# Side loads of the first feed-forward layer moved from the sync queue to GpSimd's queue

## The chip, the cores and the metric

The kernel runs on one core of a Trainium2 chip. The metric is the device time of one execution in microseconds; the number for a kernel is the median of its runs. The profile is of one execution, with the times of all instructions on TensorE (PE, and PEld for its weight loads), VectorE (DVE), ScalarE (ACT), GpSimd (POOL) and the sync engine (SP), and of the DMA transfers.

## The reference, cut to what matters

Two model blocks run one after the other on 512 tokens (and 256 context tokens) of width 1024. The part that the change touches is the end of the first layer of the first block, and the side work that is done beside it:

```python
# first layer, both token groups (768 tokens in all)
h = h + m[5] * swiglu(modulate(rms_norm(h), m[3], m[4]), w_ffn_gate[0], w_ffn_up[0], w_ffn_down[0])
# swiglu(h, g, u, d) = (silu(h @ g) * (h @ u)) @ d       widths 1024 -> 2816 -> 1024

# parameters of the NEXT layer and of the second block: they depend on the conditions alone
m = silu(cond) @ w_ada[1] + b_ada[1]           # 6 x 1024 values, for c and for c_ctx
mod = silu(c_2) @ ada_w_2[0] + ada_b_2[0]      # the same for the second block
```

All arithmetic is in 32-bit floats. The matrix products are made as three products of a high and a low part.

## The kernel before

**The feed-forward layer.** `ffn` works through 22 blocks of 128 hidden columns in groups of 4, 4, 4, 4, 4 and 2 (`FFG`). For a block it loads one tile of `wgate` and one of `wup` (512 KB each), splits each into high and low (`wsplit`: a copy on ACT, L381, and a subtraction on DVE, L389), and makes two products of 768 tokens on PE (L434, L436, L439 are the three terms). `gated` then makes silu on ACT and the product on DVE, and splits that too. After a group come the down products: four tiles of `wdown` (512 KB), each split, each used for two output blocks, which DVE adds to the residual stream (L392).

**The side work.** `ada_rows` is a generator that computes the parameters of the next layer and of the second block on DVE: 96 tiles of `wadt` (128 rows of 1024 numbers, 512 KB each) are loaded, each is multiplied by the broadcast conditions (`cb`, loaded from `crow`) and summed along the row by one `scalar_tensor_tensor` at L672, or by two for the first 16 tiles of each 48. That makes 128 such instructions. `ffn` takes steps of the generator between its products (`self.step`): two before a block's first product, two before its second, two before each output block of the down products, from block 3 on.

**Memory.** All tiles come out of one arena, which gives out what was released longest ago. A load into a tile therefore waits until the last reader of the tile that lay there is done. Those readers are mostly DVE instructions.

**Order.** The program text gives dependencies and priorities. The framework's planner writes the order of the instructions on each engine and each queue from its own estimates, so that an engine's order is not that of the text. Each engine and each queue then works strictly in the written order, and waits at the head.

**Queues.** Every load, the weights' and the side work's, is issued by SP from `load` (L404 issues, L665 issues `crow`). GpSimd issues no DMA at all; its work near this stage is some additions and subtractions of the norms just before the layer (`norm_parts`) and just after it.

Of the kernel before, what the change touches and what calls it, by code (L numbers as in the profile page):

```python
# [359 lines left out]
class _K:  # L360
# [37 lines left out]
        self.nc.sync.dma_start(b.a, src)  # L398
        return b

    def load(self, src, top=False):
        shp = list(src.shape)
        b = self.A.new(shp[1:], top=top, parts=shp[0])
        self.nc.sync.dma_start(b.a, src)  # L404
        return b

    def split_to(self, hi, lo, f32, eng=None):
# [248 lines left out]
    def ada_rows(self):  # L656


        nc, A = self.nc, self.A
        cb = [A.new([1024], top=True) for _ in range(2)]  # L660
        for l in range(1, 3):
            P = self.P[l]
            for v in range(2):
                row = 2 * (l - 1) + v
                nc.sync.dma_start(cb[v].a, self.I["crow"][row:row + 1].to_broadcast([128, 1024]))  # L665
                self.act(cb[v].a, cb[v].a, AF.Silu)
            for n in range(48):
                w = self.load(self.I["wadt"][48 * (l - 1) + n])
                vs = range(2 if n < 16 else 1)
                for v in vs:  # L670
                    t = A.new([1024])
                    nc.vector.scalar_tensor_tensor(t.a, w.a, 1.0, cb[v].a, op0=OP.mult, op1=OP.mult,  # L672
                                                   accum_out=P.a[:, n, v:v + 1])
                    t.free()
                    if v == vs[-1]:
                        w.free()
                    yield
                if n % 16 == 15:
                    r = slice(n - 15, n + 1)
                    for v in vs:  # L680
                        self.tt(P.a[:, r, v], P.a[:, r, v], self.bada.a[:, l, r], OP.add)
                        for q in (8, 32):
                            if r.start <= q < r.stop:
                                nc.vector.tensor_scalar(P.a[:, q:q + 8, v], P.a[:, q:q + 8, v], 1.0, None, op0=OP.add)
        self.free(cb)
# [107 lines left out]
    def ffn(self, l, P, T, x, a, side, rate, start=0, hook=None):  # L793
# [36 lines left out]
        for g, nb in enumerate(FFG):  # L830
# [44 lines left out]
            if last and hook:  # L875
                ws = [load(u) for u in range(4)]
                for r in parts:
                    for u in range(4):
                        down(ws[u], u, [r])
                    hook()  # L880
                self.free(ws)
            else:
                for u in range(4):
                    w = load(u)
                    down(w, u, parts if two else [(0, T)])
                    self.free(w)
# [1934 lines left out]
```

## Time and profile before

| | |
|---|---|
| median of 3 runs | 3000.76 us (2995.12 to 3003.75) |
| profiled execution, its own time | 2993.29 us |
| its span, first to last instruction | 2991.6 us |
| mean granted clock of TensorE | 0.965 of full speed |
| PE busy | 2800.4 us (94% of the span) |
| the side work's loads | issued from 566.4 to 960.0 us |

The profiled execution is one of the faster ones: its own time lies 7.5 us below the median. Times inside the trace are counted from the start of the span.

### The profile page before, as it was taken

Reading aid. Unit: us, or ns where it says so; the run is one execution under the profiler, and the core shown is the slowest. Engines: PE = TensorE matmul, PEld = TensorE weight load, DVE = VectorE, ACT = ScalarE, POOL = GpSimd, SP = SyncE. Lnnn points to the kernel's source line nnn. Section 1 sums busy time; section 2 is a strip of 40 time slices with the busy share of each in tenths; the row PEclk is TensorE's granted clock in tenths of the full one; section 3 lists DMA queues with packets and bytes.
Section 4 is the critical chain, followed back from the end, with each engine's and each line's share of the span. In section 5 each row is a group of like instructions: output and inputs, shape, how many; then the busy total and the mean of one; then the engine's idle time right before and its main releaser. Section 6 shows DMA issues by size and latency. Waiting matters only on the chain.

```text
span 2991.6 us, 43517 instructions
## 1 busy us (share of the span) xinstructions
PE 2800.4 (94%) x17924; PEld 2038.1 (68%) x17924; DVE 1684.8 (56%) x2718; ACT 1042.4 (35%) x1730; POOL 261.4 (9%) x237
## 2 busy tenths in 40 slices
PE   7989999999999999999899999989898897999997
PEld 4877557888888887665588777877675574444343
DVE  5856547776576244676765775367965754221122
ACT  4522335511211226543553532246633533011011
POOL 0034320000000000122000000010000211000000
PEclk9999999999999999999999999989998998999998
DMA  6334452356466203111322222204212136999997
GB/s 222 105 106 113 137 182 94 117 200 210 147 220 208 67 26 109 41 32 38 109 78 85 85 85 71 79 22 148 78 51 78 50 108 246 420 422 421 421 421 283
DMA packets 145271, 458.97 MB, mean 153 GB/s; under 512 B 19585, under 2 KB 49921, under 8 KB 121137
## 3 DMA queue, kind: packets, MB, share of 16 engines
q1 hardware_dynamic: 145072, 456.20, 42.8%
q8 instruction: 140, 2.29, 0.3%
q14 instruction: 59, 0.48, 0.0%
HBM read 441.36 MB, written 14.79 MB: 152 GB/s over the span
## 4 chain that ended last, share of the span: by engine, by line
PE 67%; DVE 11%; DMA 5%; issue 4%; ACT 4%; POOL 0%; SPq 0%; DVEq 0%; ACTq 0%; POOLq 0%
PE ps L434 13%; PE ps L439 13%; PE ps L436 13%; PE ps L2676 9%; DVE mem L389 7%; ACT mem L381 4%; DMA mem<-in_wadt_dram 2%; PE ps L1624 1%; DMA mem<-in_eu_dram 1%; DVE mem L392 1%; PE ps L610 1%; PE ps L1119 1%; PE ps L1932 1%; PE ps L1587 1%; PE ps L1613 1%
## 5 line engine op out<-in xcount | busy, mean ns | idle before, releaser
L381 ACT ACTIVATE mem<-mem 128x1024 fp32r<-128x1024 f32 (+15 forms) x847 | 562.2, 695 | 844.2 <-PE ps L439 216.7
L389 DVE TENSOR_TENSOR mem<-mem,mem 128x1024 fp32r<-128x1024 f32 (+17 forms) x615 | 512.5, 849 | 361.8 <-ACT mem L381 175.8
L434 PE MATMUL ps<-mem,mem 128*128 128x512 f32 (+3 forms) x1991 | 599.0, 358 | 18.5 <-ACT mem L381 14.0
L381 ACT ACTIVATE mem<-ps 128x512 f32<-128x512 f32 (+9 forms) x614 | 310.0, 518 | 830.3 <-PE ps L439 320.3
L436 PE MATMUL ps<-mem,mem 128*128 128x512 f32 (+2 forms) x1906 | 568.7, 354 | 1.1 <-DVE mem L389 1.0
L439 PE MATMUL ps<-mem,mem 128*128 128x512 f32 (+2 forms) x1977 | 419.1, 353 | 0.0
L434 PEld LDWEIGHTS ps<-mem,mem 128*128 128x128 f32 (+2 forms) x1991 | 338.3, 189 | 86.6 <-ACT mem L381 20.2
L436 PEld LDWEIGHTS ps<-mem,mem 128*128 128x128 f32 (+1 forms) x1906 | 327.2, 189 | 60.7 <-issue 6.7
L439 PEld LDWEIGHTS ps<-mem,mem 128*128 128x128 f32 (+1 forms) x1977 | 325.1, 190 | 57.0 <-issue 4.1
L436 PE MATMUL ps<-mem 128*128 128x512 f32 (+1 forms) x862 | 284.9, 359 | 1.5 <-POOL mem L389 1.0
L389 DVE TENSOR_TENSOR mem<-mem,ps 128x512 f32<-128x512 f32 (+5 forms) x234 | 134.9, 605 | 261.0 <-PE ps L2676 127.2
L434 PE MATMUL ps<-mem 128*128 128x512 f32 (+1 forms) x777 | 268.2, 369 | 14.4 <-ACT mem L381 10.9
L389 DVE TENSOR_TENSOR mem<-mem 128x512 f32<-128x512 f32 (+24 forms) x373 | 195.9, 532 | 67.6 <-ACT mem L381 21.3
L389 POOL TENSOR_TENSOR mem<-mem 128x256 f32<-128x256 f32 (+4 forms) x72 | 96.8, 1346 | 1338.6 <-ACT mem L381 903.4
L2676 PE MATMUL ps<-mem,mem 128*64 128x512 f32 x784 | 209.1, 614 | 2.1 <-DMA mem<-in_eu_dram 1.8
L389 POOL TENSOR_TENSOR mem<-mem,mem 128x512 f32<-128x512 f32 (+6 forms) x88 | 119.3, 1364 | 993.8 <-ACT mem L381 870.5
L389 DVE TENSOR_TENSOR mem<-ps,mem 128x512 f32<-128x512 f32 (+6 forms) x212 | 134.4, 647 | 115.8 <-PE ps L1111 34.8
L2676 PE MATMUL ps<-mem 128*64 128x512 f32 x688 | 183.1, 606 | 1.7 <-DMA mem<-in_eu_dram 1.7
L439 PE MATMUL ps<-mem 128*128 128x512 f32 (+3 forms) x791 | 182.1, 356 | 0.0
L436 PEld LDWEIGHTS ps<-mem 128*128 128x128 f32 x862 | 159.7, 192 | 28.7 <-issue 2.7
L434 PEld LDWEIGHTS ps<-mem 128*128 128x128 f32 x777 | 146.1, 192 | 47.4 <-ACT mem L381 16.1
L392 DVE SCALAR_TENSOR_TENSOR mem<-ps,mem,mem 128x512 f32<-128x512 f32 (+2 forms) x130 | 78.7, 654 | 144.7 <-ACT mem L381 131.1
(303 smaller groups left out, 2936.3 us busy)
## 6 DMA issues: line engine op xcount, KB each, us to landing
mem<-in_eg_dram SPq DMA_DIRECT2D x64, 1024.0 KB, 19.7
mem<-in_eu_dram SPq DMA_DIRECT2D x64, 1024.0 KB, 19.5
mem<-in_ed_dram SPq DMA_DIRECT2D x56, 1024.0 KB, 19.4
mem<-in_wadt_dram SPq DMA_DIRECT2D x96, 512.0 KB, 4.4
mem<-in_wup_dram SPq DMA_DIRECT2D x44, 512.0 KB, 3.5
mem<-in_wgate_dram SPq DMA_DIRECT2D x44, 512.0 KB, 3.5
mem<-in_wdown_dram SPq DMA_DIRECT2D x40, 512.0 KB, 3.5
mem<-in_w2in_dram SPq DMA_DIRECT2D x35, 512.0 KB, 4.0
```

The costliest lines, as they stand in the source:

```text
L381: return self.nc.scalar.activation(out, in_, func, **kw)
L389: return (eng or self.nc.vector).tensor_tensor(out, a, b, op=op)
L392: return self.nc.vector.scalar_tensor_tensor(out, a, s, b, op0=op0, op1=op1)
L434: mm(o, w(0, k), acts[k][0][:, ts], start=(k == 0), stop=False)
L436: mm(o, w(0, k), acts[k][1][:, ts], start=False, stop=False)
L439: mm(o, w(1, k), acts[k][0][:, ts], start=False, stop=(k == nk - 1))
L610: nc.tensor.matmul(b.a[32 * q:32 * q + 32, :], cs.a[:, k, :], raw.a[:, j * 512:(j + 1) * 512], start=(k == 0), stop=(k == 7))
L1119: mm(out[half[i]], vv, w.a[:, i, :], start=(J == 0), stop=(J == last))
L1587: mm(b.a[:, t0:t1], qh.a[:96, i, 128 * c:128 * c + 128], kh.a[:96, i, t0:t1], start=True, stop=True)
L1613: mm(b.a, kh.a[:97, i, ks], qh.a[:97, i, :], start=True, stop=False)
L1624: m = mm(po.a[64 * i:64 * i + 64, :], v.a[:, kb, 64 * h:64 * h + 64], pt.a[:, i, :], start=(kb == 0), stop=(kb == 5))
L2676: mm(bk.a[64 * i:64 * i + 64, 512 * n:512 * n + 512], lhs(k, i), w[i][:, k % 2, 512 * n:512 * n + 512], start=(k == 0), stop=(k == 7))
```

## The change

`load` gets an argument that says which engine issues the transfer, and `ada_rows` passes GpSimd for the 96 loads of `wadt`. The four loads of `crow` in the same function stay on SP, and so do all weight loads. Tiles, sizes and arithmetic are the same.

```diff
-    def load(self, src, top=False):
+    def load(self, src, top=False, by=None):
         shp = list(src.shape)
         b = self.A.new(shp[1:], top=top, parts=shp[0])
-        self.nc.sync.dma_start(b.a, src)
+        (by or self.nc.sync).dma_start(b.a, src)
         return b
...
             for n in range(48):
-                w = self.load(self.I["wadt"][48 * (l - 1) + n])
+                w = self.load(self.I["wadt"][48 * (l - 1) + n], by=nc.gpsimd)
```

## Rows read from the trace of the kernel before

**Rows 1.** The page, part 4: the chain that ended last, shares of the span.

```profile
PE 67%; DVE 11%; DMA 5%; issue 4%; ACT 4%; POOL 0%; SPq 0%; DVEq 0%; ACTq 0%; POOLq 0%
PE ps L434 13%; PE ps L439 13%; PE ps L436 13%; PE ps L2676 9%; DVE mem L389 7%; ACT mem L381 4%; DMA mem<-in_wadt_dram 2%; PE ps L1624 1%; DMA mem<-in_eu_dram 1%; DVE mem L392 1%; PE ps L610 1%; PE ps L1119 1%; PE ps L1932 1%; PE ps L1587 1%; PE ps L1613 1%
```

**Rows 2.** Busy time of each engine in stretches; PEclk is the granted clock.

```profile
560.00:1000.00 440.00, 429.12 (x2441) 373.27 (x2440) 286.39 (x480) 92.78 (x124) 0.00 (x0) 0.99 0.57 188
...
700.00:750.00 50.00, 44.60 (x246) 38.52 (x245) 29.75 (x51) 8.69 (x10) 0.00 (x0) 0.93 0.52 173
...
800.00:850.00 50.00, 48.23 (x275) 41.68 (x275) 39.11 (x68) 8.97 (x11) 0.00 (x0) 1.00 0.48 158
...
900.00:950.00 50.00, 46.29 (x254) 39.91 (x253) 25.36 (x41) 9.30 (x12) 0.00 (x0) 0.97 0.59 176
```

**Rows 3.** Waits of PE, 560 to 1000 us: total, times, longest.

```profile
PE ps L434 <- ACT mem L381: 10.9, 3, 5.4
```

**Rows 4.** Waits of DVE, 560 to 1000 us, the longest group.

```profile
DVE mem L672 <- DMA mem<-in_wadt_dram: 76.9, 42, 4.8
```

**Rows 5.** The chain within 690 to 735 us: start, us, what.

```profile
691.41 5.65 DMA mem<-in_wadt_dram
...
698.41 4.18 DMA mem<-in_wadt_dram
...
703.95 4.27 DMA mem<-in_wadt_dram
...
711.91 5.21 DMA mem<-in_wdown_dram
...
721.32 1.65 PE ps L434 x4
```

**Rows 6.** The whole chain's longest pieces: first and last wadt load, one wdown load.

```profile
663.76 4.68 DMA mem<-in_wadt_dram
...
918.94 4.34 DMA mem<-in_wadt_dram
925.77 4.80 DMA mem<-in_wdown_dram
```

**Rows 7.** Waits of SP's queue, 560 to 1000 us, the two longest groups.

```profile
SPq L404 <- DVE mem L672: 192.9, 90, 8.5
SPq L404 <- DVE mem L389: 137.7, 47, 14.7
```

**Rows 8.** Timeline of SP, then of DVE, in order of time around 710 us.

```profile
710.77 0.33 SPq L404 DMA_DIRECT2D mem<-in_wadt_dram  x1
711.91 0.33 SPq L404 DMA_DIRECT2D mem<-in_wdown_dram  x1
...
709.51 1.22 DVE L672 SCALAR_TENSOR_TENSOR mem<-mem,mem 128x1024 f32<-128x1024 f32 x1
...
710.66 1.22 DVE L389 TENSOR_TENSOR mem<-mem,mem 128x1024 fp32r<-128x1024 f32 x1
```

**Rows 9.** DMA issues, 560 to 1000 us, below the dots 1330 to 1800: KB, median landing.

```profile
mem<-in_wadt_dram SPq DMA_DIRECT2D x96, 512.0 KB, 4.4
mem<-in_wdown_dram SPq DMA_DIRECT2D x20, 512.0 KB, 4.5
mem<-in_wup_dram SPq DMA_DIRECT2D x18, 512.0 KB, 4.2
mem<-in_wgate_dram SPq DMA_DIRECT2D x17, 512.0 KB, 4.5
...
mem<-in_wdown_dram SPq DMA_DIRECT2D x13, 512.0 KB, 3.4
```

**Rows 10.** The tile in_wadt_dram: its issues; min, median, max ns.

```profile
L404 SPq DMA_DIRECT2D mem<-in_wadt_dram x96: 327/328/961, 566.4 to 960.0; - x96
```

**Rows 11.** Timeline of POOL, 400 to 1150 us: the neighbours of the stage.

```profile
534.53 0.74 POOL L389 TENSOR_TENSOR mem<-mem 128x256 f32<-128x256 f32 x1 [16.07 <-ACT mem L381]
1105.62 4.05 POOL L389 TENSOR_TENSOR mem<-mem 128x512 f32<-128x512 f32 x3 [570.35 <-ACT mem L381]
```

## The prediction

> **What bounds the kernel now.** Begin with the chain of work that ended last [rows 1]. PE holds 67% of it, so the kernel as a whole is bound by matrix products, but one transfer of the side work is named too: loads of `wadt` are 2% of the span, some 63 us, on the chain. The change touches just these loads, so the next view is the stage in which they run. In the busy times by stretch [rows 2] PE works 429.1 of the 440 us from 560 to 1000, DVE 286.4, POOL nothing. The stage is PE's, with 10.9 us of stalls. The waits of PE name them all [rows 3]: three, the longest 5.4 us, each ended by an ACT copy, the first half of a weight split. One more thing is lost there: in two of the three 50 us stretches that hold a stall the granted clock is 0.93 and 0.97, in the third 1.00 [rows 2]. That is 50 x 0.07 + 50 x 0.03 = 5.0 us at the lower of the two levels (1.2 instead of 2.4 GHz) after PE had stood still. So the stage loses 10.9 + 5.0 = 15.9 us, which caps any gain here.
>
> Why is the split late? The reader should follow the chain into one stall [rows 5]: three `wadt` loads in a row, one after the other through DVE's L672, then a `wdown` load, the ACT copy that ends the stall, and PE at 721.32. DVE works in its written order and stands before an L672 whose tile has not landed; the subtraction of the split, further back in its queue, stands behind it. In all DVE waits 76.9 us, 42 times, for `wadt` [rows 4]. On the whole chain there are 14 long `wadt` pieces, from 663.76 to 918.94 us, seven ahead of the first stall, three ahead of the second, four ahead of the third [rows 6].
>
> Is it the queue that makes these loads late? SP's own waits say no [rows 7]. From 560 to 1000 us it waits 137 times for DVE at L672 or L389, 330.6 us in all, while 151 loads of `wadt` and weights go out (96 + 20 + 18 + 17 [rows 9]). So nearly every load stands at the head of the queue for its own release: the memory it will land in is still being read. The timeline shows it to the hundredth [rows 8]. The L672 that starts at 709.51 ends at 710.73 and the `wadt` load goes out at 710.77; the subtraction ends at 711.88 and the `wdown` load goes out at 711.91. What is left for the queue itself is the 14 or so loads without such a wait. A loop follows: load, land, L672, release, next load. Its length, not its queue, sets DVE's pace.
>
> **The change part by part.** *Removed from SP:* 96 issues of 0.33 us [rows 10], 31.7 us of SP's time. SP waits ten times as long in that stage [rows 7], so this is worth nothing. What hides it is that waiting.
>
> The Trainium skill (DMA: Bandwidth & Descriptors, "Issuing engines are not separate DMA queues") says that transfers issued from several engines run on the same 16 DMA engines, and that a second issuing engine saves only the sequencer's time to issue. By that rule alone the change would save the 31.7 us of SP's issue time and nothing on the path, so the sum would be 2993.3.
>
> *Added to POOL:* 96 issues, each behind the same release by DVE as before, on a queue that works in order. POOL issues no DMA in this trace, so the cost must be bounded. Below stands SP's 0.33 us [rows 10], no extra delay. Above stands POOL's mean for its instructions next to the stage, 4.05 / 3 = 1.35 us for 128x512 and 0.74 us for 128x256 [rows 11], so an extra of 0.4 to 1.0 us if an issue costs POOL about what its other instructions do. I take the middle of these two, 0.7 us, because an issue by POOL is program work on that engine like the others; the ends 0 and 1.0 stay for the range. In total POOL would be busy some 96 x 1.0 = 96 us of 440, with nothing else to do: its last work ahead of the stage is at 534.53, its next at 1105.62 [rows 11]. That is the cover; without it the norms would queue behind loads that wait for DVE.
>
> The extra delay sits inside the loop. Each of the 14 `wadt` pieces on the chain grows by it, and on the chain nothing hides it: 14 x 0.7 = 9.8 us (0 to 14). For the first stall alone that is 7 x 0.7 = 4.9 us. The other 82 loads grow as well. 42 waits end at a landing [rows 4], but today 76.9 us of such waits come out as 15.9 us lost, so most of DVE's waiting is soaked up before PE sees it; I count only those on the chain.
>
> The Trainium skill (DMA: Bandwidth & Descriptors, "Specifications") gives the first byte after about 1 us for a transfer that GpSimd issues and about 0.6 us from the sync queue. By its difference of 0.4 us the chain's term would be an estimated 5.6 us and the sum 2998.8. No run here shows it yet.
>
> *Moved:* the weight loads no longer share a queue with `wadt`. A `wdown` tile lands in 4.5 us in this stage and in 3.4 us in the second layer, where no side loads run [rows 9]. The two `wdown` loads on the chain took 5.21 and 4.80 us [rows 5, 6]. If a queue of their own lets them pass, they could win 1.8 + 1.4 = 3.2 us; if the DMA engines share themselves out as before, nothing. I take half, -1.6 us. The earliest issue of a weight load does not move, since it waits for DVE's release [rows 8].
>
> *Clock:* the second stall, at 1.77 us of idle PE (48.23 of 50 us busy [rows 2]), costs no clock now. Grown by 3 x 0.7 it is 3.9 us, as long as the third, which cost 1.5 us of clock. So +1.5 (0 to 3).
>
> *Planner:* issue orders are written anew with other estimates. DVE's L672 may come earlier or later among the splits. No row prices it; the nearest are the three stalls themselves, so it can be worth anything from -15.9 to as much again. I set it to 0 for the sum.
>
> Sum, against the profiled execution's own time: 2993.3 + 9.8 - 1.6 + 1.5 = 3003.0. That execution lies 7.5 us under the median of the runs, so the median should be 3010.5; I say 3010. A difference of 0.3%, 9 us, is about what the spread of the runs shown (8.6 us) lets one tell from none.
>
> **The rivals.** *Weights set free, faster.* With the side loads away, weight tiles land like those of the second layer, 1.1 us sooner [rows 9], ahead of every split, and DVE's subtractions with them. If that keeps the first and third stall below the point where the clock drops, most of the 15.9 us comes back: -8 to -16, so medians of 2985 to 2993. For it speaks that both long stalls have a `wdown` load of about 5 us right ahead; against it that the links before that one are `wadt` loads, which gain nothing. It decides when the extra delay of a GpSimd issue is under 3.2 / 14 = 0.23 us. Chance 0.17.
>
> *Nothing passes through.* The extra delay is near the lower bound, or the new order puts L672 a little later and it waits less; losses and gains within 4 us, medians of 2997 to 3005. The stage's 440 - 286.4 = 153.6 us of idle DVE [rows 2], of which 76.9 wait for `wadt`, leave 77 us of slack that can soak it up. Against it: that slack did not prevent three stalls. Chance 0.25.
>
> *DVE's loop saturates.* If all 42 waits grow by 0.7 to 1.0 us, DVE comes 29 to 42 us later over the stage, three group boundaries take it, and half of it reaches PE: 15 to 21 us (half, because DVE regains the rest where it has slack), and with the clock's 5 us and a little more at three stalls up to 30; medians of 3016 to 3031. It decides when a boundary's delay outgrows what DVE regains until the next. One way to it would be that POOL cannot prepare an issue while DVE holds an instruction: an L672 lasts 1.22 us [rows 8] and DVE is busy 65% of the stage, so up to 0.8 us more per load on average, 14 x 0.8 = 11 us on the chain alone. The Trainium skill (SBUF — State Buffer, "SBUF: two separate sides") tells of such a lock for DVE's two-port modes, a plain fp32 copy for instance. The two kinds of instruction in [rows 8] have two inputs each and are no plain copies, so by that rule it should not strike here. Chance for the saturated loop 0.18, of which the lock 0.04.
>
> **How the numbers follow.** The forecast (+5 to +15, medians of 3006 to 3016) has 0.40. Faster by over 0.3% is the first rival and a little of the second, 0.18. Slower is the saturated loop and the part of the forecast above 3009.8, 0.18 + 0.27 = 0.45. Within 0.3% is the rest, 0.37. For 8 in 10 the range must reach into both outer rivals: from 2989, which leaves out about half of the faster case (0.08), to 3027, which leaves out the top of the saturated one (0.08) and little else. The bounds of the unknown costs, 2993.3 - 3.2 and 2993.3 + 14 + 3, are 2997.6 and 3017.8 as medians and lie inside.
>
> **What the profile of the changed kernel would show.** Right: 96 issues on POOL of about 1 us each, and landing 0.7 us later than the 4.4 us median, counted from the start of the issue; DVE's waits for `wadt` above 76.9 us by 10 to 40; PE's stalls up from 10.9 to about 19 us at the same three boundaries, at least two of the stretches with a clock below 1.00; `wdown` landing below 4.5 us; SP's waits for DVE about as long as now. Wrong: if `wadt` lands as before; if the stalls fall although it lands later (then weights did it, or the order); if DVE's order has visibly moved, so that stalls sit elsewhere; or if the time changes outside 560 to 1000 us, which no term here foresees.

## Result: slower by 0.7 to 0.9%

Timed next to the kernel before, the changed kernel takes 3023.65 us against 3002.26 us: ratio 1.0087, 95% interval 1.0064 to 1.0109. Timed once more it takes 3023.37 us against 3002.32 us: ratio 1.0066, interval 1.0046 to 1.0086. (The ratios are those recorded with the runs; the medians alone give 1.0071 and 1.0070.) So it loses some 21 us, where the forecast was 9 (3010 against 3000.76). The profiled execution has a span of 3024.4 us and a mean granted clock of 0.956.

The chain of work that ended last, on the page of the changed kernel, answers to [rows 1]. PE's share has fallen from 67% to 61%, DMA's has risen from 5% to 8%, GpSimd appears with 1%.

```profile
PE 61%; DVE 12%; DMA 8%; issue 6%; ACT 3%; POOL 1%; SPq 0%; DVEq 0%; POOLq 0%; ACTq 0%
```

Busy time by stretch of the changed kernel (columns as in [rows 2]). In the stage PE works 416.5 us instead of 429.1. PE now stalls in four 50 us stretches (the last stall lies across two of them), and the granted clock is below 1.00 in all four: 0.86, 0.97 (800 to 850), 0.98 (900 to 950) and 0.92. Before, it was so in two of three.

```profile
560.00:1000.00 440.00, 416.52 (x2352) 363.44 (x2351) 284.08 (x483) 91.28 (x122) 50.85 (x96) 0.97 0.56 189
...
700.00:750.00 50.00, 36.17 (x187) 31.00 (x186) 21.98 (x35) 8.01 (x10) 4.00 (x8) 0.86 0.49 167
...
950.00:1000.00 50.00, 47.12 (x257) 41.12 (x258) 32.80 (x61) 7.57 (x8) 5.28 (x10) 0.92 0.64 213
```

Waits in the changed kernel from 560 to 1000 us (total, times, longest), the answer to [rows 3, 4, 7]. PE's stalls are 23.5 us after 10.9, DVE's waits for `wadt` 94.8 us after 76.9. SP still waits for DVE as long as before (176.5 + 158.7 = 335.2 us after 330.6), but only 55 times, since the other waits are GpSimd's now.

```profile
DVE mem L672 <- DMA mem<-in_wadt_dram: 94.8, 50, 6.5
...
PE ps L434 <- ACT mem L381: 23.5, 4, 7.4
...
SPq L404 <- DVE mem L389: 176.5, 30, 19.4
SPq L404 <- DVE mem L672: 158.7, 25, 25.3
```

The price of one issue stands in three views. First the 96 issues by GpSimd: 0.53 us each, where SP took 0.33 [rows 10].

```profile
L404 POOL DMA_DIRECT2D mem<-in_wadt_dram x96: 527/527/727, 572.9 to 979.2; - x96
```

Then the timelines of DVE and of GpSimd near the first stall, the answer to [rows 8]. The second line of an L672, its 0.08 us read of the sum, ends at 713.72, and GpSimd's issue starts at 714.02, 0.30 us later. At 719.03 and 719.33 it is 0.30 us again. SP's issue came 0.04 us after the release [rows 8].

```profile
713.64 0.08 DVE L672 DVE_READ_ACCUMULATOR mem<-mem,mem 128x1 f32 x1
...
718.95 0.08 DVE L672 DVE_READ_ACCUMULATOR mem<-mem,mem 128x1 f32 x1
```

```profile
714.02 0.53 POOL L404 DMA_DIRECT2D mem<-in_wadt_dram  x1 [6.96 <-DVE mem L672]
719.33 0.53 POOL L404 DMA_DIRECT2D mem<-in_wadt_dram  x1 [4.78 <-DVE mem L672]
```

Last, the time from the start of an issue to the landing of the `wadt` tile, before and in the changed kernel, the answer to [rows 9]:

```profile
DMA to landing us min/median/max: 3.3/4.4/10.2
```

```profile
DMA to landing us min/median/max: 3.5/4.6/8.8
```

The median moves with what else is in flight: over all the profiles here it is 4.3 to 4.5 us with SP and 4.2 to 4.7 with GpSimd. The shortest load does not: 3.3 or 3.4 us in each of the nine profiles with SP as the issuer (in e11 of all but one), 3.5 or 3.6 in each of the nine with GpSimd. So some 0.25 us more lie behind the start of the issue, and with the 0.25 us ahead of it a turn of the loop is about 0.5 us longer. `wdown` lands in 4.1 us in the median after 4.5, which says nothing: five profiles of the kernel before have 3.9 to 4.6.

**A ruler for the stage.** Whole executions of one kernel differ by 20 us and more (2987.1 to 3008.4 us for the kernel before in one comparison). PE's instructions stand in the same order in the kernels before and after, and L481, the transposes of the norms, runs on PE just ahead of the stage and just behind it. Its row gives the first and the last start, here for the first profile of the kernel before and for the changed kernel:

```profile
L481 PE MATMUL ps<-mem,mem x10: 271/298/476, 536.0 to 1118.8; 128*128 128x128 f32 x10
```

```profile
L481 PE MATMUL ps<-mem,mem x10: 272/273/323, 542.2 to 1139.3; 128*128 128x128 f32 x10
```

The stage took 1118.8 - 536.0 = 582.8 us before and 1139.3 - 542.2 = 597.1 us after. The rest of the span behind it took 2991.6 - 1118.8 = 1872.8 and 3024.4 - 1139.3 = 1885.1 us. In these same stretches PE is busy for (first number after the length; columns as in [rows 2]):

```profile
536.00:1118.80 582.80, 569.84 (x3229) 493.88 (x3230) 354.47 (x603) 142.80 (x203) 6.05 (x6) 0.99 0.46 153
```

```profile
542.20:1139.30 597.10, 571.55 (x3230) 496.17 (x3230) 354.46 (x603) 141.92 (x203) 56.60 (x102) 0.98 0.44 149
```

The instructions are the same, so a longer busy time is what a lower clock costs them (e4 below, with a granted clock of 1.00 in its stage, needs 560.7 us for them): 1.7 us of the 14.3. The other 12.6 us are idle time. In the means of five profiles of the kernel before and two of the changed one, 16.4 us are 1.2 us of busy and 15.2 us of idle time.

The table below gives the length of the stage and of the rest for every kernel, read from the same row. (Where an edit adds lines, the numbers shift: L481 is then L482 or L484, and in e3 and e7 L672 is L676, L434 is L437, and L406 and L407 are the memset and the load.)

The orders differ too. 59 of DVE's instructions, all in the stage, stand one to four places elsewhere, L672s moved among the subtractions. So do three of ACT's, four of SP's weight loads and 19 of the 96 side loads among themselves. Outside the stage every engine's order is as it was.

### The profile page after: what moved, and what is told of

The parts are those of the page before. It is cut to its first block, busy times and chain, and to the rows that moved or that the text cites. A ratio compares the mean times of both kernels' runs of the same rounds, so it can differ in the third digit from the quotient of the medians.

```text
span 3024.4 us, 43576 instructions
## 1 busy us (share of the span) xinstructions
PE 2815.9 (93%) x17924; PEld 2049.6 (68%) x17924; DVE 1687.5 (56%) x2718; ACT 1041.6 (34%) x1730; POOL 312.6 (10%) x333
## 4 chain that ended last, share of the span: by engine, by line
PE 61%; DVE 12%; DMA 8%; issue 6%; ACT 3%; POOL 1%; SPq 0%; DVEq 0%; POOLq 0%; ACTq 0%
PE ps L434 12%; PE ps L436 12%; PE ps L439 12%; PE ps L2676 7%; DVE mem L389 7%; ACT mem L381 3%; DMA mem<-in_eu_dram 2%; DMA mem<-in_wadt_dram 2%; DVE mem L392 2%; PE ps L1624 1%; DMA mem<-in_eg_dram 1%; PE ps L610 1%; PE ps L1119 1%; PE ps L1786 1%; PE ps L1932 1%
## 5 line engine op out<-in xcount | busy, mean ns | idle before, releaser
L434 PE MATMUL ps<-mem,mem 128*128 128x512 f32 (+3 forms) x1991 | 601.4, 359 | 31.7 <-ACT mem L381 27.3
L434 PEld LDWEIGHTS ps<-mem,mem 128*128 128x128 f32 (+2 forms) x1991 | 339.1, 189 | 99.3 <-ACT mem L381 33.8
L434 PE MATMUL ps<-mem 128*128 128x512 f32 (+1 forms) x777 | 270.6, 372 | 14.9 <-ACT mem L381 11.3
L434 PEld LDWEIGHTS ps<-mem 128*128 128x128 f32 x777 | 147.4, 194 | 48.3 <-ACT mem L381 15.8
```

The lines of the kernel that those rows point to most:

```text
L434: mm(o, w(0, k), acts[k][0][:, ts], start=(k == 0), stop=False)
```

## The experiments

Four theories. **Q**: the issue by GpSimd lengthens the loop of release, issue, landing and L672. **O**: the order that the planner wrote anew costs the time. **S**: two queues at once cost something, whatever the delay. **N, later D**: part of it is variation outside the stage. (Some expectations call Q theory L, for loop, and P the theory that a queue of GpSimd's costs time behind the stage.) Medians are in us beside the kernel before in the same comparison. "Stage" is from L481 to L481, "behind" the rest of the span, each of one profiled execution.

| kernel | loads of `wadt` by | order | median, before | ratio (95%) | stage | behind |
|---|---|---|---|---|---|---|
| before, five profiles | SP | old | | | 576.6 to 582.9, mean 580.8 | 1872.8 to 1884.6, mean 1880.6 |
| changed, two profiles | GpSimd | new | 3023.4, 3002.3 | 1.0066 (1.0046 to 1.0086) | 597.1, 597.3 | 1885.1, 1883.3 |
| e1 | GpSimd | old | 3012.1, 3002.3 | 1.0027 (1.0012 to 1.0042) | 590.8 | 1883.2 |
| e2 | SP | new | 3010.1, 3002.3 | 1.0019 (1.0005 to 1.0034) | 586.1 | 1872.4 |
| e3, delay + 0.17 | GpSimd | old | 3014.2, 3000.4 | 1.0048 (1.0029 to 1.0067) | 593.8 | 1877.9 |
| e7, delay + 0.59 | GpSimd | old | 3033.5, 3002.2 | 1.0111 (1.0084 to 1.0138) | 615.8 | 1884.6 |
| e6, swapped | SP | old | 3002.3, 3000.4 | 1.0004 (0.9989 to 1.0019) | 579.3 | 1874.5 |
| e4, one scratch | SP | its own | 2984.2, 3000.4 | 0.9942 (0.9921 to 0.9964) | 562.8 | 1875.3 |
| e5, one scratch | GpSimd | its own | 2993.6, 3000.4 | 0.9966 (0.9948 to 0.9984) | 568.9 | 1882.2 |
| e9, one scratch | GpSimd | that of e4 | 2990.0, 3002.2 | 0.9961 (0.9943 to 0.9978) | 564.0 | 1882.7 |
| e8 | GpSimd | old to the first boundary | 3019.4, 3002.2 | 1.0065 (1.0042 to 1.0089) | 592.0 | 1885.0 |
| e10 | GpSimd | new to the first boundary | 3019.4, 2996.3 | 1.0071 (1.0053 to 1.0089) | 594.4 | 1883.1 |
| e11, one load | GpSimd | old | 3002.5, 3005.8 | 0.9992 (0.9969 to 1.0015) | 578.5 | 1886.8 |

One profiled execution can lie off the median of its kernel: by 12 us in e2 (2998.3 against 3010.1), by 7 in e4 (2976.8 against 2984.2) and in e7 (3040.1 against 3033.5). The whole times are the safer column.

**Both kernels again.** No edit.

> The kernel before once more, unchanged, with its own profile and against itself in five rounds, to see what one execution differs from the next by. Theory N (part of the difference of 26 us is variation outside the stage): a second profile of the unchanged kernel is shifted against the first by up to 6 us ahead of 560 us and by up to 10 us behind 1150 us, stage alone within 1 us. Against N: both profiles agree within 2 us everywhere, so that the shifts of the changed kernel outside the stage are the change's. Ratio 1.000 within 0.002 either way.

> The changed kernel once more, unchanged, with its own profile. All theories: ratio 1.007 to 1.010. In the stage PE falls behind by 14 to 16 us against the kernel before (10 at the boundary near 716 us, 2 at the second, 4 at the third). Theory N: the shifts outside the stage (+6 ahead of it, +11 between 2070 and 2400 us) come out otherwise this time; against N they come again, since they are the program's.

The kernel before against itself gives 1.0005 (0.9989 to 1.0020), so 0.15% can be told from nothing here. The stage is the same to 0.2 us in both pairs of profiles: 582.8 and 582.9 before, 597.1 and 597.3 after; three more profiles below widen the first to 576.6 to 582.9. Ahead of it and behind it the kernel before differs from itself by 7 and 12 us, so of the shifts outside the stage, part is no effect of the change.

**Queue and order, one at a time (e1, e2).** The instructions of the stage are tied in a given order by edges without semaphores. In e1 that is the old order with the loads by GpSimd, in e2 the new order with the loads by SP:

```diff
+    for seq in ORDER.values():
+        for a, b in zip(seq, seq[1:]):
+            tc.add_manual_dep(by["I-%d" % b], "I-%d" % a,
+                              mybir.DependencyInfo(mybir.DependencyClass.NoSync, mybir.DependencyReason.DATA), reason="order")
```

> The 96 loads are issued by GpSimd as in the changed kernel, but DVE, ACT, SP and GpSimd's own queue are held to the order in which the same instructions stood before, by ordering edges without semaphores. Theory Q (queue: the issue by GpSimd lengthens the loop of release, issue, landing and L672): as slow as the changed kernel, +19 to +28 us, ratio 1.0063 to 1.0095, PE's stalls in the stage 20 to 26 us. Theory O (order: what the planner rewrote costs the time): +0 to +9 us, ratio 1.000 to 1.003, stalls 11 to 17 us, though wadt lands 0.4 to 0.5 us later after its release as in the changed kernel.

> The other corner: all loads are issued by SP as before, but DVE, ACT and PE, the weights' loads among themselves and the wadt loads among themselves are held to the order in which they stand in the changed kernel. Theory Q: as fast as before, within 6 us, ratio 0.998 to 1.002, stalls in the stage 9 to 14 us. Theory O: +12 to +26 us, ratio 1.004 to 1.009, with the two stalls near 718 and 730 us of the changed kernel (7.4 and 6.4 us there).

Neither theory holds alone. The queue with the old order costs 9.8 us of 21, the order with the old queue 7.8. In the stage it is 10.0 and 5.3 against the mean of 580.8, and both together 16.4. The interval of e1 (up to 1.0042) and that of the changed kernel in the same comparison (from 1.0046) just miss each other, so the order costs something on top of the queue. PE's waits in e1, then in e2:

```profile
PE ps L434 <- ACT mem L381: 19.2, 4, 8.2
```

```profile
PE ps L434 <- ACT mem L381: 16.5, 3, 7.0
```

They stand between the 7.1 to 13.0 us of five profiles of the kernel before and the 23.5 and 27.9 of the changed kernel. The first stall of before, 5.4 us, is two in e2 (3.5 and 6.1) and two in e1 (1.7 and 8.2).

**Is it the delay (e3, e7)?** e1 with one more step in GpSimd's loop, which waits for the same release. e3 sets one column, e7 512 columns (`0:512` in place of `0:1`). The load overwrites them.

```diff
+        if touch:
+            self.nc.gpsimd.memset(b.a[:, 0:1], 0.0)
         b.ins = (by or self.nc.sync).dma_start(b.a, src)
```

> The kernel e1_gpsimd_old_order (GpSimd issues the 96 loads, all orders as before) with one more step in each loop: GpSimd first sets one column of the tile to zero, which must wait for the same release, and issues the load behind that. Theory L (loop: what counts is the time from release to landing): the delay from release to issue grows from about 0.3 us by some 0.3 to 0.6 us, so that the cost against the kernel before about doubles, from +8 to between +13 and +24 us, ratio 1.0043 to 1.008, PE's stalls in the stage 22 to 30 us after 19.2. Theory S (separation: two queues at once disturb each other, or let loads pass that were held before, whatever the delay): as e1, +5 to +12 us, ratio 1.0012 to 1.0042.

> As e3_gpsimd_old_order_dose, but GpSimd sets 512 columns of each tile to zero ahead of its load, since the one column delayed the issue by 0.17 us only (0.46 us after the release against 0.29 us in e1). The delay should grow to 0.7 to 1.2 us after the release. Theory L (the time from release to landing sets the cost): well above e1 and e3, +17 to +35 us against the kernel before, ratio 1.0057 to 1.0117, PE's stalls in the stage 26 us or more after 19.2 in e1. Theory S (it is the second queue, whatever its delay): as e1, +5 to +12 us, ratio 1.0017 to 1.004.

The dose of e3 was a small one, as GpSimd's timeline in e3 shows: DVE's release is at 710.61 (a read of 0.08 us from 710.53), the memset starts at 710.67, the load at 711.07, 0.46 us after the release. The gap between memset and load is 0.30 us here and 0.41 in other turns; the waits of GpSimd give 30.4 / 84 = 0.36 us in the mean, so a mean of 0.06 + 0.10 + 0.36 = 0.52 us after the release.

```profile
710.67 0.10 POOL L406 MEMSET mem<- 128x1 f32 x1 [3.10 <-DVE mem L676]
711.07 0.53 POOL L407 DMA_DIRECT2D mem<-in_wadt_dram  x1 [0.30 <-POOL mem L406]
```

```profile
POOL mem L407 <- POOL mem L406: 30.4, 84, 0.4
```

In e7 the release is at 711.07 (a read of 0.09 us from 710.98) and the load goes out at 711.95, 0.88 us after it:

```profile
711.13 0.53 POOL L406 MEMSET mem<- 128x512 f32 x1 [4.67 <-DVE mem L676]
711.95 0.53 POOL L407 DMA_DIRECT2D mem<-in_wadt_dram  x1 [0.30 <-POOL mem L406]
```

Against SP's 0.04 us the issue starts 0.25 us later in e1, 0.48 in e3 and 0.84 in e7. With the 0.25 us to the landing, the same in all three (3.6 us for the shortest load), a turn is 0.50, 0.73 and 1.09 us longer. The cost grows with it: 9.8, 13.8 and 31.3 us in the medians, 10.0, 13.0 and 35.0 us in the stage. That is 18 to 32 us for each microsecond of delay; whether it grows in a straight line, the intervals leave open. e3 alone can't be told from e1 (the intervals overlap), e7 can, so theory S falls as the explanation of the growth. The memsets themselves don't slow DVE: in the stage it is busy for 355.2 us in e7 and for 354.5 in the kernel before. PE's waits in e7 have reached 37.5 us, the third boundary alone 17.3:

```profile
PE ps L437 <- ACT mem L382: 37.5, 4, 17.3
```

**Swapping the queues (e6).** SP issues `wadt`, GpSimd 55 loads of weights in the stage.

```diff
-            wg = self.wsplit(I["wgate"][l, n], ("gate", n))
+            by = nc.gpsimd if l == 0 and n >= 3 else None
+            wg = self.wsplit(I["wgate"][l, n], ("gate", n), by=by)
```

> The queues are swapped: SP issues the 96 loads of wadt, GpSimd issues wgate and wup from block 3 on and wdown of the first five groups, in the old order on every engine. Two queues are in use as in e1, but the delay of an issue by GpSimd falls on the weights. Theory L: on the chain there are some 14 wadt pieces against two or three wdown pieces, so that 0.4 to 0.5 us for each gives +1 to +2 us and, with the clock, at most +5: ratio 0.999 to 1.0017. Theory S: as e1, +5 to +12 us, ratio 1.0017 to 1.004.

Theory S falls: two busy queues cost nothing here (1.9 us, within the interval), if the delay does not lie on the loads of `wadt`. The same run answers the rival of the weights set free: a queue without `wadt` beside it gains the weights nothing either (`wdown` lands in 4.4 us, within the 3.9 to 4.6 of the kernel before). The Trainium skill (DMA: Bandwidth & Descriptors, "Issuing engines are not separate DMA queues") says that a second issuing engine saves only the time that a sequencer takes to issue; this run agrees, with 0.9989 to 1.0019.

**Taking the tightness out of the loop (e4, e5, e9).** L672 writes its product, which nobody reads, to one tile that is taken once, instead of to a new tile each time. The loads then go round memory that was released longer ago.

```diff
+        t = A.new([1024], top=True)
...
-                    t = A.new([1024])
                     nc.vector.scalar_tensor_tensor(t.a, w.a, 1.0, cb[v].a, op0=OP.mult, op1=OP.mult,
                                                    accum_out=P.a[:, n, v:v + 1])
-                    t.free()
```

> All loads by SP as in the kernel before, but L672 writes its product to one tile that is taken once, instead of to a new tile for each instruction. A load then goes into memory that was released longer ago (the 128 tiles of 512 KB that the products took turn with the loads no more), so a load can be out further ahead of its L672. Theory L: DVE's waits for wadt fall well below 75 us, PE's stalls in the stage below 10.9 us, -5 to -16 us, ratio 0.995 to 0.998. Rival B (the stalls come from the bandwidth or from DVE's own load, not from the loop): within 4 us of before.

> The same with the 96 loads issued by GpSimd, in the order that the planner gives. Theory L: with the loop slack the 0.4 to 0.5 us of GpSimd cost nothing, so this is as fast as e4 within 5 us and faster than before. Theory O (the planner's order is what costs, whatever the loop): 8 us or more slower than e4. Theory S: 5 to 12 us slower than e4.

> The kernel e5_gpsimd_one_scratch (GpSimd issues, L672 writes to one tile) held to the orders of e4_sync_one_scratch on DVE, ACT, PE and among the loads. Theory L with order: the 7 us between e5 and e4 came from the order, so this is as fast as e4, -14 to -20 us against the kernel before, ratio 0.9933 to 0.9953, no stall of PE in the stage. Theory L alone: some of GpSimd's delay still shows in the loop that is left (DVE waited 37 us for wadt in e4, 54 us in e5), -7 to -13 us, ratio 0.9957 to 0.9977, one stall near 722 us.

e4 is the fastest of all: 16.2 us less than before, and PE works through the whole stage at the full clock, as its busy times show; DVE's waits for `wadt` have halved.

```profile
560.00:1000.00 440.00, 440.00 (x2552) 385.14 (x2551) 295.98 (x489) 97.33 (x130) 0.00 (x0) 1.00 0.57 190
```

```profile
DVE mem L672 <- DMA mem<-in_wadt_dram: 37.3, 15, 4.6
```

So neither the bandwidth nor DVE's load made the stalls: both are at least as high here (190 GB/s after 188, DVE busy for 296.0 us after 286.4). The edit changes memory and the planner's order together, so that the looser loop, and not the other order, ended the stalls is argued and not shown. With GpSimd in its own order (e5) one stall of 3.6 us is left, and the whole time is 9.4 us above e4's: the expectation of theory L, within 5 us, was missed. In the order of e4 (e9) one stall of 1.2 us is left. In the stage e9 lies 1.2 us above e4, e5 6.1 us, with one profile each. In the whole time e9 is 4 to 6 us above e4 (each against the kernel before), as the expectation had it in which some of GpSimd's delay still shows; the intervals overlap, so whether the queue's 10 us have shrunk to that or to nothing is not settled.

**Where the order costs (e8, e10).** The old order up to the first boundary and the new one behind it, and the other way round; both by edges as in e1.

> GpSimd issues the 96 loads; DVE, ACT and GpSimd's queue are held to the old order up to the first boundary (716 us), behind it they keep the order that the planner wrote for the changed kernel. If the order's cost lies ahead of the first boundary: stalls there near 10 us as in e1 (13.8 and 14.6 in the two profiles of the changed kernel), total +8 to +14 us, ratio 1.0027 to 1.0047. If it lies behind it: stalls of the third boundary 7 to 11 us as in the changed kernel (6.5 in e1) and a total of +15 to +26 us, ratio 1.005 to 1.0087.

> The complement of e8: GpSimd issues the 96 loads; up to the first boundary every queue keeps the order that the planner wrote for the changed kernel, behind it the order of the kernel before. If the order's 12 us between e1 and the changed kernel arise ahead of the first boundary: stalls there 13 to 15 us, the third 6 to 7 us, total +15 to +24 us, ratio 1.005 to 1.008. If they arise behind it: first boundary near 10 us, total +6 to +12 us, ratio 1.002 to 1.004. If both halves carry some: +12 to +17 us.

Not settled. By the ruler each half carries a part (1.2 and 3.6 us above e1, of 6.4). The whole times, +17.2 and +23.1 us, put both kernels next to the changed one: e8 then says that the order's cost arises behind the first boundary, e10 that it arises ahead of it. A single profile of the kernel before varies by 6 us in the stage, so these differences are too small for it.

**Behind the stage (e11).** One of the 96 loads by GpSimd, all orders old, and more profiles of the kernel before.

```diff
-                w = self.load(self.I["wadt"][48 * (l - 1) + n])
+                w = self.load(self.I["wadt"][48 * (l - 1) + n], by=nc.gpsimd if l == 1 and n == 40 else None)
```

> One of the 96 loads is issued by GpSimd, the other 95 by SP, all orders as in the kernel before. The question is the time behind the stage, from the last L481 at its end to the end of the span: 1883 to 1885 us in the two profiles of the changed kernel, and 1872.8 and 1884.6 us in the two of the kernel before. If a queue of GpSimd's in the program is enough to cost there (theory P): 1882 to 1885 us behind the stage, the stage itself 582 to 584 us between the L481 on either side. If it is the chance of two dips of the clock (theory D): 1872 to 1877 or 1882 to 1885 us, as in the looks at the kernel before.

> One more look at the kernel before. Stage between the L481 on either side 582.7 to 583.1 us in every look. Theory P: 1872 to 1876 us behind it in most looks, the 1884.6 of the second profile the exception. Theory D: some looks of each kind.

> As the look before this one: the share of looks with 1872 to 1876 us behind the stage is what tells P from D.

> One more look of the same kind: under theory D some of the looks have 1882 to 1885 us behind the stage, under theory P hardly any.

Theory D: the three profiles of the kernel before have 1880.9, 1882.7 and 1882.0 us behind the stage, so the 1872.8 of its first profile is the exception, not the 1884.6 of the second. e11 has 1886.8, within no theory's range, and costs nothing in the whole time. From the means 3.6 us are left between changed and before (1884.2 - 1880.6); whether the change makes them is open. These profiles also moved the base of the stage: 580.4, 576.6 and 581.1 us, not 582.7 to 583.1 as expected, which is why the mean of five is used.

## Why the prediction was right and wrong

The direction was the likelier one, and 3023.5 lies in the range, below its top of 3027. But the change came out more than twice as large as forecast. By the ruler the 21 us are made up so: queue 10.0 us (e1), order 6.4 us on top of it (597.2 - 590.8), behind the stage 3.6 us, sum 20.0. The two parts of the stage are read off one profile of e1, where the kernel before alone spreads over 6 us, so their sizes are rough.

**"I set it to 0 for the sum"** (the planner) is the step that failed. The text had named the bounds, -15.9 to as much again, and took the middle without a row for it. The order cost 6.4 us in the stage, and in the whole time about 21.1 - 9.8 = 11.3 us beside the queue. e2 shows that it costs time without GpSimd too, with an interval just above 1. With 11 us for it the forecast of 9 would have been 20. Which of the moved instructions does it is open.

**"14 x 0.7 = 9.8 us"** came out at 10.0 us, by luck: two errors cancelled. The delay is not 0.7 but about 0.5 us, one half ahead of the start of the issue (0.29 or 0.30 us after the release instead of 0.04) and one half between there and the landing. The multiplier is not 14 but 20 in e1, and 18 to 32 over the three delays. I had counted the `wadt` pieces on the chain and taken DVE's other waits for soaked up; that count is no fixed number either (9 to 18 on the chains of the five profiles of the kernel before, 560 to 1000 us). The rival of the saturated loop lets all 42 waits of DVE for `wadt` [rows 4] grow and half of it reach PE; with the measured delay that is 42 x 0.5 / 2 = 10.5 us. That the waits work this way was not shown. Its range, 3016 to 3031, holds the measured time, but by a delay that was too large and without the order.

The Trainium skill (DMA: Bandwidth & Descriptors, "Specifications") has a difference of 0.4 us to the first byte. No profile line here gives a first byte; measured is about 0.5 us from the release to the landing. The 5.6 us estimated from it were too little, since the multiplier was 14 there too.

**Weights, -1.6 us:** nothing shows it. `wdown` at 4.1 us lies within what the kernel before shows, and e6, where the weights have a queue of their own as well, gains nothing, so the rival "set free" falls. **SP's time, 0:** right, by the same run. **Clock, +1.5 us:** right in size. The granted clock did fall in more stretches, but most of that lies in time in which PE stood still anyway: the busy time of the same instructions grew by 1.7 us (569.84 to 571.55), in the means by 1.2. What grew is the idle time, by 12.6 and 15.2 us.

**Lock between DVE and GpSimd (0.04):** nothing speaks for it. The issues take 527 to 727 ns, and e7's memset of 711.13 runs beside an L672 (711.10 to 712.33) and takes 0.53 us like the mean of the 96.

**The signs that were named:** DVE's waits up by 17.9 us (10 to 40 forecast), stalls 23.5 (about 19), a clock below 1.00 in at least two stretches and SP's waits as before came. An issue takes 0.53 us, not about 1.0, and `wadt` lands 0.2 us later in the median, not 0.7, which comes near the sign "lands as before" that was to prove the text wrong. The stall at the first boundary became two; that was named as the sign of a moved order, but it is none here, since e1 in the old order has two as well (1.7 and 8.2 us). Time outside 560 to 1000 us, the last sign of being wrong, stays open with the 3.6 us.

## What to carry to other kernels

When a load waits for the instruction that frees its memory, an engine that reacts later pays on every turn of that loop: measure both halves of the delay, ahead of the issue and up to the landing, and count the waits at the landing, not only the pieces on the critical chain. Before the queue is changed, look at why the loop is tight; here a scratch tile took turns with the loads, and one fixed tile in its place (with the other order that came with it) gave 16 us with SP. Where a planner writes the order, an edit of the queue is also an edit of the order, and one run with the old order held fast separates the two.

## What was not expected of the hardware

GpSimd reacts to a release quickly, but not with a load: in e3 its memset starts 0.06 us after DVE's release, while its load starts 0.30 us after DVE's release in the changed kernel, and 0.30 us after its own memset in e7, 0.30 or 0.41 in e3. Loads that follow one another without a wait have no such gap: three from 698.92 us in e1 take 1.57 us, as long as three issues. So the quarter of a microsecond belongs to the start of a load that had to wait, and not to the signal from DVE; why GpSimd needs it is not shown. The second quarter, between the start of the issue and the landing (3.5 or 3.6 us at the least instead of 3.3 or 3.4), comes on top.
